# A two-level Strassen MLP on one core: first matmul in a written order of parts, sums begun in PSUM, second level in four products

## The chip, the core and the metric

The kernel runs on one core of one Trainium2 chip. The metric is the device time of one launch in microseconds (us); of three runs of the kernel before, the median was 1485.96 us (1485.87 to 1487.07). The profile shown below is one more execution of the same program, with the span between its first and last instruction.

## What is computed

```python
x: (8, 1024, 1024)   w1: (1024, 4096)   w2: (4096, 1024)      # float32
h = x @ w1
h = 0.5 * h * (1 + np.tanh(np.sqrt(2 / np.pi) * (h + 0.044715 * h ** 3)))
return (h @ w2).astype(np.float32)
```

An MLP block: 8192 rows, a first matmul with a hidden width of 4096, GELU, a second matmul. Operands are cast to float16, sums are kept in float32.

## The kernel before

**Tiling.** The 8192 rows go in eight stages (`sb` 0 to 7) of 1024 rows. A stage is `matmul1` (x times w1, GELU, result kept in SBUF as four blocks `g11, g12, g21, g22`) and then the second matmul (`matmul2_made` in stages 0 and 1, `matmul2` from stage 2 on). Each matmul is a Strassen-Winograd product over a 2x2 split of its operands: seven products of half-size blocks, named 1 to 7, instead of eight. The operands of the products are blocks or sums of blocks; the tables `W_SUM` and `S_SUM` say which. In the second matmul of stages 2 to 7 every product is itself split once more in the same way (class `Inner`, 7 x 7 parts), so its matmuls are 256 columns wide instead of 512.

**First matmul.** The hidden width is walked in eight pairs `j` of two 128-column chunks (`h` = 0 and 1). A pair has the seven products, each 4 matmuls of 512 columns for each chunk, 8 in all. From stage 2 on, products 2 and 3 (`INNER_1`) have a second level: seven parts of two 256-column matmuls, 14 in all, named here by their part `r`. The sums of the rows that this needs (`xs.inner[2]`, `xs.inner[3]`) are made on VectorE (DVE), four additions for each product; for product 3 that is done in the first pair (`more`). The matching sums of w1 were made in stage 1 (`inner_sums`), stored in DRAM (`in1_d`), and come back with the pair's other operands in `StoredHalf`, nine loads of 256 KB for each pair.

**How a pair's result is put together.** Product 1 goes to bank A and ScalarE (ACT) copies it to SBUF (`a`). Product 2 goes to its own bank, or part by part to a bank `z`, and DVE adds it to `a`, part by part (five or six additions of 256 columns) and then once more for each chunk. Product 6 is accumulated on bank A, ACT copies A again (`t`), product 7 is accumulated on A and added to the copy `p5` of product 5, product 4 is accumulated on A, and product 3 is added to `t`. ACT applies GELU to each of the four results of each chunk. At the end DVE subtracts g11 - g21 for the second matmul (`difference`).

**What sets the order.** TensorE (PE), ACT and DVE instructions are pinned to the order in which the Python code writes them (`keep_in_program_order`), so each of these engines is a queue: an instruction that waits holds up what stands behind it. All matmuls are issued from few lines: L438 (first matmul), L910 (`Inner.multiply`), L951 (`matmuls2`). All additions of DVE are issued from `tt` (L119), ACT's copies from `act_copy` (L135), GELU from L451. Loads go through SyncE's DMA queue (SP), stores and the cast of the next rows through GpSimd's (POOL). PSUM has 8 banks, taken by `psum()`; the framework lets one engine at a time into a bank, in the written order, and a new tile gets one when an old tile's last reader is done. SBUF tiles come from pools: `up` (26 tiles named `u`), `gcp` (4 named `gc`), `tp` (named `tmp`).

**Stage 1** has no second level in its first matmul. While it runs, DVE makes the next quarter's w1 sums (`MadeQuad.sum`, `inner_sums`), POOL stores them, and the raw blocks of the next quarter are read back by the four loads of `MadeQuad.__init__` (L168). These DVE jobs were run after the pair's own work: in pair 0 all of them behind the last addition of the pair (`half = 3 if j % 2 else 0`).

**End of a second matmul.** `FILL_2` makes the next stage's row sums on DVE while PE works; the last of them is `n3` (`37:n3`), run after product 3's last step, so it ends when the next first matmul has already begun. `i2` makes `xs.inner[2]` (`46:i2`).

Of the kernel before, what the change touches and what calls it, by code (L numbers as in the profile page):

```python
# [8 lines left out]
F32 = mybir.dt.float32  # L9
DT = mybir.dt.float16  # L10
GT = mybir.dt.float16
GELU = mybir.ActivationFunctionType.Gelu_apprx_tanh
ADD = mybir.AluOpType.add
# [8 lines left out]
SUMS = tuple(W_SUM)  # L22
BLOCKS = ("11", "21", "12", "22")
STEPS = (1, 2, 6, 5, 7, 3, 4)
INNER_1 = (2, 3)
HALF_ORDER = (1, 2, "s2", 5, 6, 3, "s3", 7, 4)
SPLIT_IN_M1 = (2, 3)


def slots(table):  # L30
# [6 lines left out]
    ;50:w60 w61;51:w62 w63;52:g30 g31;53:g32 g33  # L37
    ;60:w70 w71;61:w72 w73;62:w40 w41;63:w42 w43
    ;73:x5;40:x7 x6;41:x3 q5;42:q6 q7 q4
    ;43:i2 i3""".replace("\n    ", "")),  # L40
    slots("""10:g60 w50;11:g61 w51;12:g62 w52;13:g63 w53
    ;20:g50 p55;21:g51 p56;22:g52 p57;23:g53 p54
    ;50:w60 w61;51:w62 w63;52:g30 g31;53:g32 g33
# [12 lines left out]
    ;61:n5;63:a77;64:a76;65:a75;66:a73;67:n7  # L56
    ;71:y11 y12;72:y21 y22;73:a37;74:a36 w11;75:a35 w12;76:a33 w21;77:w22
    ;31:z11 z12;32:z21 z22;36:n6;37:n3""".replace("\n    ", ""))


@with_exitstack
def kernel(
# [27 lines left out]
    up = ctx.enter_context(tc.tile_pool(name="up", bufs=26))  # L90
    gp = ctx.enter_context(tc.tile_pool(name="gp", bufs=1))
    gcp = ctx.enter_context(tc.tile_pool(name="gcp", bufs=4))
    tp = ctx.enter_context(tc.tile_pool(name="tp", bufs=10))
    consts = ctx.enter_context(tc.tile_pool(name="consts", bufs=1))
    dram = ctx.enter_context(tc.tile_pool(name="dram", bufs=1, space=bass.MemoryType.DRAM))
    xdram = ctx.enter_context(tc.tile_pool(name="xdram", bufs=2, space=bass.MemoryType.DRAM))
# [3 lines left out]
    w2v = w2.rearrange("(a c p) (b o) -> b a p c o", a=2, p=P, b=2)  # L100

    w1_d = [dram.tile([P, 4, KH * QW], DT, name=f"w1_d{q}") for q in range(NI // QC)]
    in1_d = [dram.tile([P, 2, 2, KH * 2 * P], DT, name=f"in1_d{q}") for q in range(NI // QC)]
    raw_d = [dram.tile([P, 4, KH * QW], DT, name=f"raw_d{q}") for q in range(NI // QC)]
    in_d = {m: dram.tile([P, 4, NI // 2, OH // 2], DT, name=f"in_d{m}") for m in range(1, 8)}
    w2_d = [dram.tile([P, 4, QC * OH], DT, name=f"w2_d{q}") for q in range(NI // QC)]
# [2 lines left out]
    def psum():  # L109
        return pp.tile([P, HT], F32, name="ps")  # L110

    def temp():
        return tp.tile([P, HT], F32, name="tmp")

    def unit(rows, cols):
        return up.tile([P, rows, cols], DT, name="u")
# [1 line left out]
    def tt(out, in0, in1, op, pin=False):  # L118
        i = nc.vector.tensor_tensor(out=out, in0=in0, in1=in1, op=op)  # L119
        if pin:  # L120
            tc.keep_in_program_order(i)
# [12 lines left out]
    def act_copy(out, in_):  # L134
        tc.keep_in_program_order(nc.scalar.copy(out=out, in_=in_))  # L135
# [23 lines left out]
    class MadeQuad:  # L159


        def __init__(self, q, first, store):
            self.q, self.first, self.store = q, first, store
            self.raw = {b: unit(2 * KH, 2 * P) for b in BLOCKS}
            self.ops = {m: self.raw[b] for m, b in W_TERM.items()}
            if not first:
                for b in ("12", "11", "22", "21"):
                    nc.sync.dma_start(out=flat(self.raw[b]), in_=raw_d[q][:, BLOCKS.index(b), :])  # L168
# [44 lines left out]
                nc.gpsimd.dma_start(out=w1_d[self.q][:, SUMS.index(m), :], in_=flat(self.ops[m]))  # L213

        def inner_sums(self, m):
            t = self.ops[m].rearrange("p (h k c) (e n) -> p h k c e n", h=2, k=2, e=2)
            s = up.tile([P, 2, 4, 2, P], DT, name="u")

            def operand(b):
                if isinstance(b, int):  # L220
                    return s[:, :, list(S_SUM).index(b)]
                return t[:, :, int(b[1]) - 1, :, int(b[0]) - 1, :]

            for j, (u, op, v) in S_SUM.items():
                tt(operand(j), operand(u), operand(v), op, True)
            nc.gpsimd.dma_start(
                out=in1_d[self.q][:, INNER_1.index(m)].rearrange("p h n -> p (h n)"),
                in_=s.rearrange("p h j c n -> p (h j c n)"),
            )

        def chunk(self, m, c):
            return columns(self.ops[m], c % QC)
# [5 lines left out]
    def stored(d, raw, m):  # L238
        return raw[:, BLOCKS.index(W_TERM[m]), :] if m in W_TERM else d[:, SUMS.index(m), :]

    class StoredHalf:


        def __init__(self, i):
            q, h = divmod(i, 2)
            self.ops, self.sums = {}, {}
            n = KH * 2 * P
            for k, m in enumerate(HALF_ORDER):
                if k % 2 == 0:
                    two = up.tile([P, 2, n], DT, name="u")  # L250
                t = two[:, k % 2]
                if isinstance(m, str):
                    m = int(m[1])
                    self.sums[m] = t.rearrange("p (j c n) -> p j c n", j=4, c=2)
                    d = in1_d[q][:, INNER_1.index(m), h]
                else:
                    self.ops[m] = t.rearrange("p (k n) -> p k n", k=KH)
                    d = stored(w1_d[q], raw_d[q], m)[:, h * n:(h + 1) * n]
                nc.sync.dma_start(out=t, in_=d)

        def chunk(self, m, c):
            return self.ops[m][:, :, c % 2 * P:(c % 2 + 1) * P]

    class XOps(dict):
# [16 lines left out]
            for job in self.inner_jobs(m):  # L281
                job()

        def inner_jobs(self, m):
            self.inner[m] = up.tile([P, 4, 2, HT // 2], DT, name="u")

            def operand(b):
                if isinstance(b, int):
                    return self.inner[m][:, SUMS.index(b)]
                k, t = int(b[0]) - 1, int(b[1]) - 1  # L290
                return self[m][:, 2 * k:2 * k + 2, t * HT // 2:(t + 1) * HT // 2]

            return [lambda j=j, s=s: tt(operand(j), operand(s[0]), operand(s[2]), s[1], True)
                    for j, s in W_SUM.items()]

    def x_blocks():
        return {b: unit(KH, HT) for b in ("22", "21", "12", "11")}
# [8 lines left out]
    class First:  # L306
# [26 lines left out]
            load_in_order(flat(self.rows[a, q]), x2[r0:r0 + P, :])  # L333

        def cast(self, a, q):
            xn = tp.tile([P, 2, HT], DT, name="tmp")
            tc.keep_in_program_order(nc.vector.tensor_copy(out=xn, in_=self.rows[a, q]))
            self.rows[a, q] = xn

# [73 lines left out]
    def x_cast_paced(s, g_chunk, q, xb):  # L413

        mark = nc.gpsimd.tensor_copy(out=pace, in_=g_chunk[:, :2])  # L415
        return x_cast(s, mark, range(q * P, (q + 2) * P, P), xb)
# [15 lines left out]
    def matmul1(xs, sb, quads, start=None):  # L432
# [109 lines left out]
        for j in range(NI // 2):  # L542
# [10 lines left out]
                continue  # L553
            jobs = list(ahead(j))
            banks_a = [psum(), psum()]
            a = [temp(), temp()]
            for h in range(2):
                product(banks_a[h], source, 1, cs[h], True)
                act_copy(a[h], banks_a[h])
            banks_c, p5, t = [], [], [temp(), temp()]  # L560

            def five(h):
                if len(p5) == h:
                    banks_c.append(psum())
                    p5.append(temp())
                    product(banks_c[h], source, 5, cs[h], True)
                    act_copy(p5[h], banks_c[h])

# [108 lines left out]
        blocks = nxt.get("blocks")  # L677
        return g, early, nxt.get("xb") if blocks is None else XOps(blocks)

    def store(sb, b, q, src, **kw):
# [16 lines left out]
    def matmul2_made(sb, g, keep_w1, xb):  # L699
# [74 lines left out]
        def post(m, q, bank):  # L774
            if m in (1, 5, 6):
                t = {1: a, 5: p5, 6: t6}[m]
                t[q] = temp()
                act_copy(t[q], bank)
            elif m == 4:
                c = temp()  # L780
                act_copy(c, bank)
                store(sb, "21", q, c)
            else:
                t = {2: a, 3: t6, 7: p5}[m][q]
                tt(t, t, bank, ADD, True)
                at[q] = store(sb, {2: "11", 3: "12", 7: "22"}[m], q, t)
# [8 lines left out]
        for m, name, first in (  # L795
            (1, "a", True), (2, "b", True), (5, "c", True), (6, "a", False),
            (3, "c", False), (7, "a", False), (4, "a", False),
        ):
            for q in range(NQ):
                if first:  # L800
                    banks[name].append(psum())
                bank = banks[name][q]
                matmuls2(bank, s2[q] if m == 6 else rows(g[operands[m]], q), pieces(m), first)
                post(m, q, bank)
                if (m, q) == (5, 0) and sb == 0:
                    xb = x_cast(sb + 1, nc.gpsimd.tensor_copy(out=pace, in_=p5[0][:, :2]))
                if (m, q) == ((5, 0) if sb else (6, NQ - 1)):
                    xs = XOps(x_transpose(xb, load_in_order))
                    keep("22")
                if (m, q) == (3, NQ - 1) and sb == 0:  # L810
                    quad = MadeQuad(0, False, True)
                if (m, q) == (4, 0) and sb:
                    quad = StoredHalf(0)
                if (m, q) == (1, NQ - 1) and sb == 0:
                    sums[5] = [unit(2, HALF) for _ in range(NI // QC)]
                    for t in sums[5]:
                        act_copy(t[:, 0, :1], warm)
                    bring("22", act_copy, True)
                    keep("21")
                    keep("12")  # L820
                run((m, q))
# [206 lines left out]
            for n in products[m].steps(into[m]):  # L1028
                run((m, n))

    idle = consts.tile([P, HT], DT, name="idle")
    nc.vector.memset(idle, 0.0)
    warm = consts.tile([P, 1], F32, name="warm")
    pace = consts.tile([P, 2], DT, name="pace")
# [2 lines left out]
    first = First()  # L1037
    xs, quads = first.xs, [first.quad]
    for sb in range(NSB):
        g, early, nxt = matmul1(xs, sb, quads, first if sb == 0 else None)  # L1040
        if sb < 2:
            xs, quads = matmul2_made(sb, g, None if sb else quads[-1].keep_raw, nxt)
            continue
        matmul2(sb, g, early, nxt)
        if nxt is not None:
            xs, quads = nxt, [StoredHalf(0)]


# [28 lines left out]
```

## Time and profile before

| | us |
|---|---|
| median of three runs | 1485.96 |
| span of the profiled execution | 1485.0 |
| PE busy, of the span | 1476.1 |
| DVE busy | 1146.3 |
| ACT busy | 613.5 |
| POOL busy | 225.3 |
| first matmul of stage 2, its 544 matmuls (from 402.7) | 94.0 |
| first matmul of stage 4 (762.2 to 856.3), PE busy | 94.04 |
| the same, DVE busy | 68.66 |
| the same, ACT busy | 60.14 |
| DMA: read 355.47 MB, written 111.15 MB, over the span | 314 GB/s |

A page of the profile has for each engine the time in which it was busy; PE's time counts overlapping matmuls once. The view of chains follows what ended last back from step to step; a line there is a start, a length and a group of instructions. The timeline merges equal instructions that follow each other; a bracket tells how long the engine was idle before and what ended that. In the view of groups a row has a shape, its count, total time and the mean of one in ns. In the matmul groups the mean is longer than the spacing of two matmuls, because they are pipelined; the spacing is read from long stretches in the chain.

### The profile page before, as it was taken

The page shows a single profiled execution, that of the slowest core. Times are in us where ns is not written, and L with a number is a line of the kernel's source. Part 1 is how long each engine was busy: PE and PEld are TensorE (multiplying, and loading weights), DVE is VectorE, ACT ScalarE, POOL GpSimd, SP SyncE. Part 2 cuts the span into 40 slices and gives each one's busy share as a digit, 9 for nine tenths or more (in the row PEclk, how much of TensorE's full clock was granted, in tenths as well). Part 3 has the DMA queues.
Part 4 walks back from the last instruction along what each step waited for, and adds up shares of the span by engine and source line. Part 5 has one row for each costly group of instructions (what it writes and reads, how often), then busy time and mean ns, then how long its engine had stood idle before and what let it go on. Part 6 is the DMA issues. An engine that isn't in the chain of part 4 may idle for free.

```text
span 1485.0 us, 26324 instructions
## 1 busy us (share of the span) xinstructions
PE 1476.1 (99%) x9879; PEld 962.5 (65%) x9879; DVE 1146.3 (77%) x1792; ACT 613.5 (41%) x1154; POOL 225.3 (15%) x311
## 2 busy tenths in 40 slices
PE   8999999999999999999999999999999999999998
PEld 4444444444455787558875588655886568855687
DVE  5657458767677899779987799877997779877787
ACT  5665126621166412663136621366214652056510
POOL 1541122222201012100022001210111101101011
PEclk9999999999999999999999999999999999999999
DMA  9999898987997999999999999998999989997886
GB/s 323 345 345 394 224 360 287 405 274 228 379 292 169 359 304 309 319 214 387 325 295 337 218 372 313 307 305 234 376 292 326 303 263 341 295 370 245 295 277 213
DMA packets 242719, 453.70 MB, mean 306 GB/s; under 512 B 80672, under 2 KB 85792, under 8 KB 241696
## 3 DMA queue, kind: packets, MB, share of 16 engines
q1 hardware_dynamic: 215680, 358.69, 71.6%
q0 software_dynamic: 26912, 93.34, 21.5%
q8 instruction: 77, 1.26, 0.3%
q14 instruction: 50, 0.41, 0.1%
HBM read 355.47 MB, written 111.15 MB: 314 GB/s over the span
## 4 chain that ended last, share of the span: by engine, by line
PE 96%; DMA 2%; DVE 1%; ACT 0%; SPq 0%; issue 0%; DVEq 0%
PE ps L438 48%; PE ps L910 35%; PE ps L951 13%; PE ps L368 1%; DVE tmp L119 1%; DMA gc<-in_w_dram 1%; DMA u<-in_d 1%; DMA u<-w_d 1%; DMA u<-raw_d 0%; ACT tmp L135 0%; SPq L132 0%; PE ps L345 0%; DVE u L196 0%; DVE u L119 0%; DVE u L356 0%
## 5 line engine op out<-in xcount | busy, mean ns | idle before, releaser
L438 PE MATMUL ps<-u 128*128 128x512 f16 (+1 forms) x4104 | 746.6, 344 | 0.5 <-DMA u<-w_d 0.2
L119 DVE TENSOR_TENSOR tmp<-tmp,ps 128x256 f32<-128x256 f32 (+1 forms) x930 | 450.8, 532 | 263.3 <-PE ps L438 166.5
L438 PEld LDWEIGHTS <-u 128*128 128x128 f16 x4104 | 400.8, 98 | 343.7 <-issue 9.4
L135 ACT COPY tmp<-ps 128x512 f32<-128x512 f32 x410 | 231.2, 581 | 300.1 <-PE ps L438 153.9
L451 ACT ACTIVATE g<-tmp 128x512 f16<-128x512 f32 x378 | 238.1, 633 | 162.8 <-DVE tmp L119 162.7
L910 PE MATMUL ps<-u,gc 128*128 128x256 f16 x2688 | 300.4, 273 | 0.0
L910 PEld LDWEIGHTS <-gc 128*128 128x128 f16 x2688 | 262.5, 98 | 31.2
L119 DVE TENSOR_TENSOR u<-u 128x2048 f16<-128x2048 f16 (+3 forms) x292 | 217.8, 785 | 21.2 <-DMA raw_d<-u 11.4
L910 PE MATMUL ps<-u,g 128*128 128x256 f16 x2016 | 227.9, 273 | 0.0
L135 ACT COPY u<-ps 128x512 f32<-128x512 f32 (+1 forms) x134 | 78.0, 587 | 348.9 <-PE ps L910 341.4
L910 PEld LDWEIGHTS <-g 128*128 128x128 f16 x2016 | 197.3, 98 | 24.1
L119 DVE TENSOR_TENSOR u<-u,ps 128x512 f32<-128x512 f32 x216 | 147.8, 684 | 34.7 <-PE ps L910 28.5
L697 POOL DMA_DIRECT2D out_dram<-u x70 | 64.0, 989 | 710.5 <-issue 366.0
L951 PE MATMUL ps<-u,g 128*128 128x512 f16 x768 | 166.4, 379 | 0.0
L951 PEld LDWEIGHTS <-g 128*128 128x128 f16 x768 | 75.2, 98 | 90.6
L119 DVE TENSOR_TENSOR g<-g,g 128x2048 f16<-128x2048 f16 (+1 forms) x136 | 128.8, 969 | 1.6 <-ACT g L451 1.6
L119 DVE TENSOR_TENSOR gc<-g,gc 128x2048 f16<-128x2048 f16 x84 | 102.4, 1219 | 0.6
L119 DVE TENSOR_TENSOR gc<-g 128x2048 f16<-128x2048 f16 x78 | 95.0, 1218 | 0.0
L451 ACT ACTIVATE g<-ps 128x512 f16<-128x512 f32 x134 | 79.9, 597 | 15.1 <-PE ps L438 7.9
L138 POOL CAST u<-gc 128x1024 f16<-128x1024 f32 x40 | 45.4, 1141 | 69.5 <-DMA gc<-in_w_dram 56.4
L536 POOL TENSOR_TENSOR gc<-g 128x2048 f16<-128x2048 f16 x6 | 24.4, 4063 | 61.9 <-ACT g L451 61.9
L415 POOL COPY pace<-g 128x2 f16<-128x2 f16 x24 | 4.4, 185 | 190.1 <-ACT g L451 190.1
(37 smaller groups left out, 249.3 us busy)
## 6 DMA issues: line engine op xcount, KB each, us to landing
u<-w_d SPq DMA_DIRECT2D x336, 256.0 KB, 6.6
u<-in_d SPq DMA_DIRECT2D x168, 512.0 KB, 7.1
u<-raw_d SPq DMA_DIRECT2D x252, 256.0 KB, 7.1
out_dram<-u POOLq DMA_DIRECT2D x70, 512.0 KB, 9.2
gc<-in_w_dram SPq DMA_DIRECT2D x48, 512.0 KB, 6.3
u<-in_d SPq DMA_DIRECT2D x96, 256.0 KB, 6.8
raw_d<-u SPq DMA_DIRECT2D x32, 512.0 KB, 8.7
u<-raw_d SPq DMA_DIRECT2D x32, 512.0 KB, 13.9
```

What stands on the lines that cost most here:

```text
L119: i = nc.vector.tensor_tensor(out=out, in0=in0, in1=in1, op=op)
L135: tc.keep_in_program_order(nc.scalar.copy(out=out, in_=in_))
L138: pool_last[0] = nc.gpsimd.tensor_copy(out=out, in_=in_)
L368: tc.keep_in_program_order(nc.tensor.matmul(bank[:, cols], lhsT=w[:, k, :], rhs=self.xs.blocks[f"{a}{r}"][:, k, cols], start=r == 1 and k ...
L415: mark = nc.gpsimd.tensor_copy(out=pace, in_=g_chunk[:, :2])
L438: tc.keep_in_program_order(nc.tensor.matmul(bank, lhsT=w, rhs=x, start=first and k == 0, stop=k == n - 1, skip_group_check=not first,))
L451: gelu_last[0] = nc.scalar.activation(out=g[b][:, c, :], in_=src, func=GELU)
L536: nc.gpsimd.tensor_tensor(out=early[7], in0=u, in1=v, op=SUB)
L697: return nc.gpsimd.dma_start(out=rows, in_=src, **kw)
L910: tc.keep_in_program_order(nc.tensor.matmul(bank[:, i * OH // 2:(i + 1) * OH // 2], lhsT=t[:, c, i * P:(i + 1) * P], rhs=self.y[j][:, c, : ...
L951: tc.keep_in_program_order(nc.tensor.matmul(pair(bank), lhsT=a[:, c, :], rhs=chunks(pieces[c // QC])[:, :, c % QC, :], start=(first and c ...
```

## The change

Stage 0 keeps `matmul1`. Stages 1 to 7 use a new function, `matmul1_seeded`, which takes its order from written tables: `ORDER_PLAIN` in stage 1, and from stage 2 on `ORDER_HEAD` for pair 0, `ORDER` for pairs 1 to 6, `ORDER_TAIL` for pair 7. An entry is an operation and a key; all pairs' entries are sorted by 1000 j + key, so that pairs overlap: part 5 of product 1 (`P1r5`) of a pair comes at key -255, before the end of the pair ahead. `Pmchb` is half b (two matmuls of 512 columns) of product m for chunk h, `Pmrn` is part n (two matmuls of 256 columns) of a product with the second level, `J` runs jobs of DVE from a list until 1.2 of their written costs are used up, `gxyh` is a GELU.

Products 1, 5, 2 and 3 now have the second level (`INNER_1 = (1, 5, 2, 3)`), but in the pair of `ORDER_HEAD` only product 2. Sums no longer go through SBUF where a bank can hold them: ACT or DVE writes the start of a sum into a bank, and the matmuls that follow accumulate on it (`skip_group_check`, `start=False`). Of w1's second-level sums only those of products 1 and 2 are stored in DRAM (`STORED_1`); those of 3 and 5 are made by POOL from the loaded operands (`make_sums`), eight additions of 128x256 for each pair, issued when the pair before begins. POOL also takes over `difference`. In stage 1 the second-level sums of the first quarter move from the end of stage 0 (`43:i2 i3` of `FILL`) into pairs 0 and 1. `temp` tiles become pairs of half the number.

```diff
-INNER_1 = (2, 3)
-HALF_ORDER = (1, 2, "s2", 5, 6, 3, "s3", 7, 4)
+INNER_1 = (1, 5, 2, 3)
+STORED_1 = (1, 2)
...
+ORDER_PLAIN = order("""P1c10:-104 P1c11:-46 P1c00:-14 P1c01:13 P5c00:22 J:62 J:97 J:142 b1:167 J:222 b0:227 P5c10:233
+    P5c01:272 J:307 P5c11:313 p51:342 P6c10:395 P6c11:407 w1:413 p50:424 P6c00:424 P6c01:461 w0:499
+    P2c00:511 P2c10:513 P2c01:526 P3c10:550 J:556 P3c00:564 P3c01:616 J:672 P7c00:704 P7c10:715
...
+ORDER_HEAD = order("""J:-1385 P1c10:-1332 P1c11:-1168 J:-1152 P1c00:-1041 P1c01:-1039 a1:-953 P2r5:-773 a0:-627 P2r1:-592
+    P5c00:-480 P5c10:-400 P5c01:-302 P6c00:-240 P6c01:-196 J:-160 P6c10:-111 J:-106 p50:170 acc_2:211
+    q11_2:227 P2r6:278 P5c11:303 J:330 P6c11:342 w0:343 P3c00:354 q12_2:356 J:405 P3c01:417 p51:429
...
+ORDER = order("""P1r5:-255 P1r1:-201 q11_1:-134 P1r2:-80 s5_1:-76 P1r6:-72 P5r5:-7 q12_1:6 P5r1:10 P1r7:18 P1r3:20
+    q11_5:166 s5_5:184 P5r2:194 P5r6:195 q2x_1:195 P1r4:203 a0:204 P2r5:204 q12_5:225 P6c00:229 P5r7:236
...
+        def make_sums(self):
+            for m, s in self.sums.items():
...
+                for j, (u, op, v) in S_SUM.items() if m not in STORED_1 else ():
+                    tc.keep_in_program_order(nc.gpsimd.tensor_tensor(
+                        out=operand(j), in0=operand(u), in1=operand(v), op=op
+                    ))
...
+        bank_of = {1: "A", 6: "A", 7: "A", 4: "A", 2: "B", 5: "C", 3: "C"}
+        out_of = {"11": "B", "12": "C", "21": "A"}
...
+                if plain:
+                    self.source = quads[j // 2]
+                    self.jobs = ahead(j) + splits.pop(j, [])
+                    return
+                for i in range(len(quads), min(j + 3, npair)):
+                    quads.append(StoredHalf(i, table(i)))
...
+                if j == 0:
+                    for m in INNER_1:
+                        if m not in xs.inner:
+                            pool = (gcp, "gc") if m in (1, 5) else (up, "u")
+                            self.jobs += [(0.42, job) for job in xs.inner_jobs(m, *pool)]
...
+            def add(self, what, m):
+                m = int(m)
+                z, name = self.z[m], bank_of[m]
+                if m in (1, 5):
+                    i = 1 if m == 1 else 2
+                    if what == "s5":
+                        act_copy(seed[:, i], z[:, right])
+                    elif what == "q11":
+                        act_copy(self.bank(name, 0)[:, left], z[:, left])
+                    base = {"q12": seed[:, i], "q2x": seed[:, 0:i + 1:i]}
+                else:
+                    t = self.tmp("a" if m == 2 else "w")
+                    if what == "acc":
+                        tt(t[:, :, right], t[:, :, right], twice(z[:, right]), ADD, True)
+                    base = {"q11": t[:, 0, left], "q12": t[:, 0, right], "q2x": pair(t[:, 1])}
...
+                if what == "q2x":
+                    tt(pair(self.bank(name, 1)), base[what], twice(z[:, left]), ADD, True)
+                else:
+                    half = left if what == "q11" else right
+                    tt(self.bank(name, 0)[:, half], base[what], z[:, left], ADD, True)
...
+            def move(self, what, h):
+                if what == "p5":
+                    act_copy(self.tmp("p5")[:, h], self.bank("C", h))
+                    return
+                A = self.bank("A", h)
+                if what == "a":
+                    act_copy(self.tmp("a")[:, h], A)
+                elif what == "b":
+                    act_copy(self.bank("B", h), A)
+                else:
+                    p5 = self.tmp("p5")[:, h]
+                    out = p5 if what == "v" else self.tmp("w")[:, h] if 3 in self.inner else self.bank("C", h)
+                    tt(out, p5, A, ADD, True)
...
+        def ahead(j):
+            q, second = divmod(j, 2)
+            jobs = []
+            if j < 2:
+                jobs += quads[0].inner_jobs(STORED_1[j])
...
+            if not second:
+                quads.append(MadeQuad(q + 1, False, True))
+            quad = quads[q + 1]
+            jobs += [(1.2, lambda m=m: quad.sum(m, pin=True)) for m in ((7, 4) if second else (5, 6))]
+            jobs += quad.inner_jobs(STORED_1[second])
+            return jobs
```

## The prediction

> **What bounds the kernel now.** I read the shares of the engines, then the chain that ended last in order of time, then DVE's timeline where the chain leaves PE, then the rows by shape, then the loads of stage 1.
>
> ```profile
> PE 1476.1 (99%) x9879; PEld 962.5 (65%) x9879; DVE 1146.3 (77%) x1792; ACT 613.5 (41%) x1154; POOL 225.3 (15%) x311
> PE 96%; DMA 2%; DVE 1%; ACT 0%; SPq 0%; issue 0%; DVEq 0%
> ```
>
> PE is busy for 99% of the span and holds 96% of the chain: taken-away matmuls shorten the span, and every new wait of PE lengthens it.
>
> ```profile
> 209.28 96.69 PE ps L438 x448
> ...
> 496.70 85.63 PE ps L910 x784
> ...
> 588.83 1.96 DVE tmp L119 x4
> 590.79 0.04 issue
> 590.83 24.92 PE ps L438 x145
> ...
> 770.78 85.54 PE ps L438 x494
> 856.32 85.63 PE ps L910 x784
> ...
> 950.47 85.54 PE ps L438 x494
> ```
>
> Dense stretches give the spacing: 96.69/448 = 0.2158 us for a matmul of 512 columns, 85.63/784 = 0.1092 for 256. The stage from 770.78 to 950.47 takes 179.69. Its matmuls fill 320 x 0.2158 + (224 + 784) x 0.1092 = 179.1, so 0.55 us of a stage is gaps (one stage has 0.26 more, 590.83 to 770.78).
>
> ```profile
> 762.99 1.22 DVE L119 TENSOR_TENSOR u<-u 128x2048 f16<-128x2048 f16 x1
> 764.33 0.42 DVE L119 TENSOR_TENSOR tmp<-tmp,ps 128x256 f32<-128x256 f32 x1
> 764.67 0.88 DVE L119 TENSOR_TENSOR u<-u 128x512 f16<-128x512 f16 x2
> 765.90 0.75 DVE L119 TENSOR_TENSOR u<-u 128x512 f16<-128x512 f16 x2
> ```
>
> The first matmul of stage 4 begins at 762.11 (PE's timeline), but DVE is still at `n3` until 764.2, 2.0 us later with the overlap of its pipeline. Then come, one by one, four jobs of `xs.inner[3]`, 1.45 us in sum.
>
> **The change part by part.**
>
> *Matmuls.* A product on the first level costs 8 x 0.2158 = 1.727, on the second 14 x 0.1092 = 1.529: 0.198 less. In pairs 1 to 7 products 1 and 5 gain it (14 times), in pair 0 product 3 loses it: 13 x 0.198 = 2.57 a stage, stages 2 to 7: **-15.4**. Stages 0 and 1 keep their matmuls.
>
> *Old gaps.* They come from additions at places that the new order no longer has: 6 x 0.55 + 0.26: **-3.6**.
>
> *ACT and DVE in a middle pair.* Rows by shape:
>
> ```profile
> L119 DVE TENSOR_TENSOR tmp<-tmp,ps 128x512 f32<-128x512 f32 x402 | 260.3, 683 | 139.2 <-PE ps L438 78.2 <-PE ps L951 35.0 <-ACT tmp L135 14.7
> L135 ACT COPY tmp<-ps 128x512 f32<-128x512 f32 x410 | 231.2, 581 | 300.1 <-PE ps L438 153.9 <-PE ps L951 140.9 <-issue 1.7
> L119 DVE TENSOR_TENSOR tmp<-tmp,ps 128x256 f32<-128x256 f32 x528 | 200.4, 417 | 124.1 <-PE ps L438 88.3 <-ACT tmp L135 35.0
> L536 POOL TENSOR_TENSOR gc<-g 128x2048 f16<-128x2048 f16 x6 | 24.4, 4063 | 61.9 <-ACT g L451 61.9
> ```
>
> A pair becomes 3 x 1.727 + 4 x 1.529 = 11.30 us of PE. DVE had 11 additions of 256 and 6 of 512 columns and `difference`; it gets 6 and 10, by the rows 6 x 0.42 + 10 x 0.68 = 9.3. ACT has 8 GELUs, 4 copies of 512, 4 of 256: under 9. Both fit under 11.3, so what counts is the way back to PE. I walked the order of one pair with these durations. A matmul's result comes 0.16 after its slot (379 - 216 ns) and a hand-off takes 0.05. The tightest: `P1r6`, then `q12_1` on DVE, then `P1r7`, which writes the bank that `q12_1` reads: 0.16 + 0.42 + 0.05 = 0.63, covered by `P4c00`, `P5r5`, `P5r1` = 0.87. `P1r1`, `q11_1` on ACT, `P1r2`: at most 0.8 with the 512 row for the unseen copy of 256, covered by 1.09. So the walk has no wait, with 0.2 us to spare. No row has DVE or ACT writing PSUM. Bounds: below, the duration of the rows (PSUM read costs DVE nothing: 683 ns here against 686 from SBUF alone); above, a second access in series, the row's whole 0.42. I take the row, with one small gap of 0.05 for each of the 42 pairs, as each pair has now: **+2.1**. Banks: `z` and A, B, C live 83 us in sum for each pair (A alone 16 and 18), 83/11.3 = 7.3 of 8; in the walk a bank comes free just in time.
>
> *POOL and the loads.* A pair keeps its nine loads of 256 KB (pair 0 has eight), SP's queue is as long as before. POOL gets eight additions of 128x256 by 4063/2048 ns an element: 0.51 each, at most 0.7 with the 0.18 of POOL's smallest copy: 5.6; `difference` at half the 4.06 row: 2.0. Together 7.6 of 11.3, begun a pair ahead, so the pair ahead covers it: nothing on the path. In pair 0, where the cover is short, `s5` is made from a load that lands 11 to 12 us after the start, three additions later (14) just when `P5r5` of pair 1 comes (11.0 + 2.7). The casts of the next rows (L410), which stand behind `make_sums` in POOL's queue, go out some us later; their rows are wanted four pairs on. If an addition took over 1.1, POOL would set the pair.
>
> The trace shows POOL and DVE in each other's way: POOL's cast of 1024 columns is 1.04 alone and 1.38 to 1.50 while DVE adds SBUF to SBUF (28.0 to 37), and DVE's additions from PSUM keep their 0.68. In the new first matmuls of stages 2 to 7, DVE adds SBUF to SBUF only in pair 0. [...]
>
> *Pair 0 of stages 3 to 7.* `INNER_1` minus `i2` puts twelve row sums into the `J` entries, and all four filled `J` stand before `acc_2` and `q11_2` on DVE. DVE: free at 2.0, twelve jobs 3 x 1.45 = 4.4, `acc_2` 0.6, `q11_2` 0.4: done at 7.4. PE stands before `P2r6`, which writes the bank that `q11_2` reads, after ten halves of products 1, 5 and 6 (10 x 0.4316) and two parts (2 x 0.218): 4.75. Wait 2.7, nothing can pass it: **5 x 2.7 = +13.5**. Stage 2 has `i2`, `i3` from stage 1, eight jobs and a DVE that is free from the start: no wait (were DVE as late there as in stage 4, 1.2). In stages 3 to 7 the loads of pair 1 land 9 to 11 us after the start; `P1r1` of pair 1, now after 8.4 + 2.7, only just finds them, so less work on DVE alone would not win all of the 2.7 back.
>
> *Pair 0 of stage 1.* `J:97` holds `sum(5)` of the next quarter, `J:142` `sum(6)`; both stand before `w1`. They need raw blocks issued from 197.82 on, the second landing after 18.1 us, the third after 19.3:
>
> ```profile
> L168 SPq DMA_DIRECT2D u<-raw_d x4: 320/368/601, 197.8 to 201.6; - x4
> DMA to landing us min/median/max: 15.7/18.7/19.3
> ```
>
> Issued at 198.33 and 199.14 they land at 216.4 and 218.4, 7.1 and 9.1 after the stage's first matmul (209.28). Before, these sums ran behind the pair. One store of 512 KB less runs beside them (`i3` moves to pair 1); I take 0.6 off. DVE: `sum(5)` 6.5 to 7.65, `sum(6)` 8.5 to 9.65, four sums 1.35, `w1` 0.68: 11.7. PE wants `P3c10` (its bank is written by `w1`) after 15 halves, 6.5. Wait 5.2; bounds 0 (blocks there in time) and 5.9 (no store saved): **+5.3** with the hand-off. Pairs 2 and 4 have the same pattern, but their blocks are issued when buffers come free, in pair 1 and 3, and DVE runs 1.7 us ahead: 0 taken, 3 each as the bound.
>
> *Clock.* At the start the seven matmuls on `idle` (1.19 to 4.36) are spaced 0.43, half speed, and from 4.25 on the granted clock is 1.0; gaps up to 1.2 us between 4 and 13 did not lower it. A wait of 5.3 is longer than any gap the trace has after that. Bounds 0 and 3.2 at half speed, 1.6 lost; I take **+1.0**. [...]
>
> Sum against the profile's own span: 1485.0 - 15.4 - 3.6 + 2.1 + 13.5 + 5.3 + 1.0 = 1487.9. The median of the runs stands 1.0 above that span: **1489 us**.
>
> **Rivals.**
>
> *Stage 1 doesn't wait* (the raw blocks land early): it decides if the third block is there 3.3 us after the start, so that `sum(6)`, four sums and the end of `P6c11` leave `w1` done at 6.5; then 1489 - 6.3 = 1482.7. For it: these loads are not pinned, the framework may issue them sooner; against it: what stands before them in SP's queue is unchanged, and their 15.7 to 19.3 us are time in that queue. With half the head's wait gone too, 1476.
>
> *Hand-offs set the middle pairs.* The place is `P1r6`, `q12_1`, `P1r7` and its likes in 42 pairs; the price: DVE and ACT writing PSUM, or Tile's choice of banks, cost over 0.2 us more for each hand-off. Below that it is nothing. With 0.3, seven places of a pair are 0.1 to 0.26 late, 1.0 us a pair, 42 us; with 0.2, about 0.5 a stage, 3. For it: 7.3 of 8 banks, two waits on most instructions. Against it: reading PSUM costs the rows nothing. Likely size if it comes: +10, 1499; slower than before.
>
> *POOL late* (over 1.1 for an addition): each 0.1 above costs 0.8 a pair, 34 us in all. Against it: the 4063 row.
>
> *The change does not shorten PE*, because weight loads limit 256 columns: excluded by 0.1092 over 784 matmuls.
>
> **How the numbers follow.** My case, 1483 to 1494, likeliest 1489: 0.5. Stage 1 or pair 0 better than that, below 1483: 0.22. Hand-offs or banks: 0.2; POOL or loads: 0.08. A change within 0.2% (3.0 us, 1483.0 to 1488.9) can't be told from none; my case has half of itself on each side of 1489: same 0.26, slower 0.52, faster 0.22. Range 1477 to 1502; my case's own is 1483 to 1494.
>
> **What would show it.** Right: in each of stages 3 to 7 one PE gap of 2.5 to 3 us, 4.8 us after its first matmul, released by DVE; in stage 1 one gap near 215.7 released by DVE, which waits for `raw_d`; pairs 1 to 6 at 11.3 us each. Wrong: gaps in the middle pairs released by ACT or DVE, PE waiting for POOL, or no gap in stage 1.

## The result, and the profile after

The changed kernel takes 1502.1 us (median of 4 runs, 1499.1 to 1503.8) against 1486.5 before: a ratio of 1.0103, 95% interval 1.0089 to 1.0118. It is slower. The forecast was 1489 with a range up to 1502, so the time lies at the very top of it, and above the 1494 where the forecast's own case ended. The profiled execution is the shortest of the four: a span of 1497.3, which is 12.3 more than before.

The page first (engines' shares, then the chain by engine), and from the view of waits the line of PE's longest group: total, times, longest.

```profile
PE 1467.9 (98%) x10347; PEld 1011.6 (68%) x10347; DVE 1169.4 (78%) x1672; ACT 606.7 (41%) x1210; POOL 560.1 (37%) x703
PE 79%; DVE 4%; DMA 1%; issue 1%; SPq 0%; DVEq 0%
```

```profile
PE ps L821 <- DVE ps L152: 20.4, 9, 4.6
```

PE held 96% of the chain before and holds 79% now. All long waits of PE in these matmuls are for DVE: nine, of 20.4 us. Five of them are the ones in pair 0 of stages 3 to 7, four lie in stage 1. The timelines of PE, DVE and POOL in stage 1 (start, length, engine, operation, and in brackets the idle time before it and its releaser):

```profile
208.50 6.64 PE L821 MATMUL ps<-u 128*128 128x512 f16 x30
219.76 13.93 PE L821 MATMUL ps<-u 128*128 128x512 f16 x56 [4.62 <-DVE ps L152]
234.85 24.50 PE L821 MATMUL ps<-u 128*128 128x512 f16 x112 [1.16 <-DVE ps L152]
260.24 24.50 PE L821 MATMUL ps<-u 128*128 128x512 f16 x112 [0.89 <-DVE ps L152]
...
213.60 1.23 DVE L152 TENSOR_TENSOR u<-u 128x2048 f16<-128x2048 f16 x1 [6.37 <-DMA u<-raw_d]
216.41 2.69 DVE L152 TENSOR_TENSOR u<-u 128x2048 f16<-128x2048 f16 x5 [1.58 <-DMA u<-raw_d]
...
229.63 2.90 DVE L152 TENSOR_TENSOR u<-u 128x512 f16<-128x512 f16 x2
...
230.10 2.14 POOL L903 TENSOR_TENSOR g<-g,g 128x1024 f16<-128x1024 f16 x1
```

The wait that ends at 219.76 is the one forecast: `sum(5)` and `sum(6)` stand still until their raw blocks land. The one that ends at 234.85, in pair 1, is another: two additions of 0.42 us take 2.90, the second of them 2.56, and POOL's `difference` runs inside that.

Stages 3 to 7 in the chain of waits (start, length, what):

```profile
596.34 86.44 PE ps L821 x598
775.68 88.03 PE ps L821 x598
956.62 88.03 PE ps L821 x598
```

Each piece begins where the wait before `P2r6` ends, and each has the same 598 matmuls. The first takes 86.44, the others 1.59 more. Windows show why (busy time of PE, PEld, DVE, ACT and POOL, then the granted clock, `PEclk`, where 0.50 is half clock, then DMA's share and GB/s):

```profile
772.82:776.23 3.41, 0.84 (x6) 0.40 (x5) 3.38 (x10) 0.00 (x0) 0.00 (x0) 1.00 1.04 417
776.23:779.64 3.41, 3.41 (x12) 1.38 (x10) 1.03 (x2) 1.01 (x2) 1.08 (x2) 0.50 1.04 388
779.64:783.06 3.42, 3.42 (x24) 2.21 (x23) 1.90 (x3) 1.92 (x5) 3.34 (x6) 1.00 1.05 400
591.90:595.30 3.40, 1.87 (x9) 0.77 (x8) 3.33 (x11) 0.59 (x1) 0.00 (x0) 1.00 1.04 416
595.30:598.70 3.40, 2.36 (x14) 1.35 (x14) 2.61 (x6) 0.80 (x2) 0.00 (x0) 1.00 1.04 409
```

In stage 4 the whole wait of 2.73 us lies in 772.82 to 776.23, and the next 3.41 us run at half clock: 12 matmuls where 24 follow. In stage 3 the same wait is split between two such stretches, and the clock stays. The half-clock stretches of this execution begin at 776.23, 957.13, 1138.04 and 1318.95: 53 times 3.413 us apart, a fixed grid.

The parts in sum, where a matmul's slot is the spacing of two in a dense stretch (0.2158 and 0.1092 us) and a wait is counted from the end of the last slot:

| part of the span | forecast | in this execution |
|---|---|---|
| matmuls (sum of slots 1470.0 to 1454.6) | -15.4 | -15.4 |
| five waits before `P2r6` | +13.5 | +13.65 |
| half clock after them, 4 x 1.68 | 0 | +6.7 |
| stage 1, pair 0 | +5.3 | +4.78 |
| half clock after it | +1.0 | +1.7 |
| stage 1, odd pairs | 0 | +3.9 |
| old gaps, small gaps | -3.6 + 2.1 | -3.0 (what is left) |
| sum | +2.9 | +12.3 |

### The profile page after: what moved, and what is told of

The parts are those of the page before. It is cut to its first block, busy times and chain, and to the rows that moved or that the text cites. A ratio compares the mean times of both kernels' runs of the same rounds, so it can differ in the third digit from the quotient of the medians.

```text
span 1497.3 us, 27850 instructions
## 1 busy us (share of the span) xinstructions
PE 1467.9 (98%) x10347; PEld 1011.6 (68%) x10347; DVE 1169.4 (78%) x1672; ACT 606.7 (41%) x1210; POOL 560.1 (37%) x703
## 4 chain that ended last, share of the span: by engine, by line
PE 79%; DVE 4%; DMA 1%; issue 1%; SPq 0%; DVEq 0%
PE ps L821 40%; PE ps L1192 33%; PE ps L1233 6%; DVE u L152 2%; DMA u<-w_d 1%; DVE gc L152 1%; DVE tmp L152 0%; DVE ps L152 0%; SPq L318 0%; DVEq L152 0%
## 5 line engine op out<-in xcount | busy, mean ns | idle before, releaser
L821 PE MATMUL ps<-u 128*128 128x256 f16 (+1 forms) x3508 | 627.6, 328 | 20.4 <-DVE ps L152 20.4
L152 DVE TENSOR_TENSOR tmp<-tmp,ps 128x512 f32<-128x512 f32 x352 | 238.1, 685 | 127.6 <-PE ps L821 50.3
L168 ACT COPY tmp<-ps 128x512 f32<-128x512 f32 x282 | 163.8, 588 | 309.6 <-PE ps L821 150.8
L892 ACT ACTIVATE g<-ps 128x512 f16<-128x512 f32 x336 | 197.9, 601 | 106.4 <-PE ps L821 105.8
L329 POOL TENSOR_TENSOR u<-u 128x256 f16<-128x256 f16 x336 | 216.4, 670 | 51.6 <-DMA u<-w_d 19.5
L152 DVE TENSOR_TENSOR ps<-tmp,ps 128x256 f32<-128x256 f32 (+1 forms) x298 | 154.7, 532 | 38.4 <-PE ps L821 30.8
L903 POOL TENSOR_TENSOR g<-g,g 128x1024 f16<-128x1024 f16 x56 | 122.0, 2179 | 159.2 <-ACT g L892 159.1
L152 DVE TENSOR_TENSOR ps<-seed,ps 128x256 f32<-128x256 f32 (+1 forms) x168 | 94.5, 563 | 71.7 <-PE ps L821 69.3
L821 PE MATMUL ps<-gc,u 128*128 128x256 f16 x672 | 120.4, 273 | 0.0
L152 DVE TENSOR_TENSOR gc<-g,gc 128x2048 f16<-128x2048 f16 x84 | 114.0, 1357 | 3.1 <-PE ps L1192 3.1
```

What stands on the lines that cost most here:

```text
L329: tc.keep_in_program_order(nc.gpsimd.tensor_tensor(out=operand(j), in0=operand(u), in1=operand(v), op=op))
L821: tc.keep_in_program_order(nc.tensor.matmul(out, lhsT=w, rhs=x, start=first, stop=True, skip_group_check=not first,))
L892: gelu_last[0] = nc.scalar.activation(out=g[b][:, self.cs[h], :], in_=src, func=GELU)
L903: nc.gpsimd.tensor_tensor(out=g["21"][:, cs], in0=g["11"][:, cs], in1=g["21"][:, cs], op=SUB)
```

## The experiments

All are edits of the changed kernel; times are medians, "under" is against its 1502.1.

**head_fill.** Work in the wait, nothing else: `keep_clock` issues matmuls of 512 columns on zeros into a bank that nobody reads.

```diff
                 elif o[0] == "P":
+                    if self.j == 0 and o == "P2r6" and sb > 2:
+                        keep_clock(psum(), 12)
```

> Twelve matmuls of 512 columns on zeros, into a bank that nobody reads (no part of the computation), stand before P2r6 in pair 0 of stages 3 to 7: 12 x 0.216 = 2.6 us of work in the wait of 2.73. The order of everything else stays. Theory (the wait itself halves the clock): the wait for DVE ends at the same time (P2r6 within 0.2 us of 7.5 us after the stage's start), the half-clock stretches of 3.41 us after it in stages 4 to 7 are gone, the profile's span is 4 x 1.7 = 6.8 us under 1497.3, and the median, if ordinary runs drop the clock in all five stages and now and then elsewhere, 7 to 12 under 1502.1, with runs closer together than 1499.1 to 1503.8. Rival A (the clock falls for another reason, for example the load of the stage's start as a whole): the stretches stay, time as after or up to 2 us more. Rival B (no bank is free for them): P2r6 comes later by up to 2.6 us in each stage, time 1500 to 1510.

Measured: 1494.5 (1492.6 to 1495.2), ratio to before 1.0053 [1.0038, 1.0068], 7.6 under. PE's timeline in stage 4:

```profile
772.00 4.92 PE L823 MATMUL ps<-u 128*128 128x512 f16 x24
776.75 2.75 PE L375 MATMUL ps<-seed 128*128 128x512 f16 x12
779.48 3.62 PE L823 MATMUL ps<-u 128*128 128x256 f16 x20
```

`P2r6` comes 7.5 us after the stage's start as before (768.20 to 775.68 there), the real work waits as long, and no half-clock stretch is left in stages 2 to 7. So the wait made the clock fall, and the clock alone is worth 7.6 us in the median, about what four or five stretches of 1.7 give. The profiled span, 1493.4, is only 3.9 under, not the 6.8 expected: in this execution pair 0 of stage 1 waits 7.60 where it was 4.78, and half clock there lasts 10.24 us where it was 3.41.

**fill_some.** The same with `(2, 3, 4, 5, 6)[sb - 3]` matmuls in place of 12.

> Matmuls on zeros (no part of the computation) fill part of the wait of 2.73 us before P2r6: 2, 3, 4, 5 and 6 of 0.216 us in stages 3 to 7, so that 2.3, 2.1, 1.9, 1.65 and 1.45 us stay idle. Theory (the clock is judged in stretches of 3.41 us on a fixed grid, and the stretch after one that had more than about half of it idle runs at half clock; seen so far: 1.71 idle kept the clock, 2.20 lost it): stages 3 and 4 lose 3.41 us of clock if their idle time lies in one stretch of the grid, stages 6 and 7 lose none whatever the phase. Rival (the length of the wait counts, 2.7 us or more, not the grid): none of the five is at half clock. Rival (any wait over 1.4 us): all five are.

Measured (one execution): 1496.5. The windows of the grid around the waits of stages 3 and 4:

```profile
596.30:599.71 3.41, 1.40 (x7) 0.53 (x6) 3.38 (x10) 0.29 (x1) 0.00 (x0) 1.00 1.03 414
599.71:603.13 3.42, 3.30 (x9) 1.28 (x9) 1.79 (x4) 0.58 (x1) 0.49 (x1) 0.50 1.04 401
777.21:780.62 3.41, 1.65 (x8) 0.67 (x7) 3.36 (x9) 0.33 (x1) 0.00 (x0) 1.00 1.04 416
780.62:784.04 3.42, 3.26 (x20) 1.87 (x20) 2.42 (x5) 1.18 (x2) 0.61 (x1) 1.00 1.04 407
```

Of the five waits only stage 3's loses the clock. By the matmuls' slots (0.216 and 0.109 us) its stretch had 2.18 us without work; the highest that kept the clock was 2.14, in stage 1 of this execution, and stage 4 had 1.92. The stretches of the other kernels agree: 1.71 kept it, 2.20 and more lost it. Both rivals fall: a wait of 2.30 us was enough, one of 2.08 was not. No limit on the length of a wait fits, since the 2.73 of the changed kernel's stage 3, split by the grid, kept the clock. The expected "about half" was too low a limit: of 3.41 us, 2.14 without work kept the clock and 2.18 lost it.

**head_late.** Six row sums ahead of `q11_2` in place of twelve.

```diff
-... P6c01:-196 J:-160 P6c10:-111 J:-106 p50:170 ... P5c11:303 J:330 P6c11:342 ... q12_2:356 J:405 P3c01:417
+... P6c01:-196 P6c10:-111 p50:170 ... P5c11:303 P6c11:342 ... q12_2:356 P3c01:417
```

> Pair 0 of stages 2 to 7 keeps six row-sum jobs ahead of acc_2 and q11_2 instead of twelve; the other six run behind q2x_2 (entries J:584 and J:690). Theory (DVE's job list makes the wait, and a wait of 2.73 us also halves the granted clock for one stretch of 3.41 us): DVE reaches q11_2 2.2 us earlier, the wait before P2r6 falls from 2.73 to about 0.5 us, and no half-clock stretch is left in stages 4 to 7: span 5 x 2.2 + 4 x 1.7 = 17.8 us under the 1497.3 of the changed kernel's profile, about 1480; the median 18 to 22 under 1502.1. Rival A (the loads of pair 1, landing 9 to 11 us after the stage's start, come to the top): a new wait of 1 to 2.5 us before P1r5 or P1r1 of pair 1 in each of these stages, time 1490 to 1497. Rival B (DVE's late start from the stage before makes the wait, not the jobs): the wait stays over 2 us.

Measured: 1489.5, ratio 1.0019 [1.0009, 1.0028], 12.6 under. The wait before `P2r6` is 0.59 to 0.69, no clock is lost there: the theory is right on the cause, and rival B is out. Its size, 18 to 22 under, was missed: some 6 to 7 us later a second wait of 0.73 to 1.05 us has come, 4.5 us in five stages. In stage 6 the timelines of DVE and POOL show it:

```profile
1133.39 2.49 DVE L152 TENSOR_TENSOR u<-u 128x512 f16<-128x512 f16 x4
...
1134.07 2.97 POOL L329 TENSOR_TENSOR u<-u 128x256 f16<-128x256 f16 x4 [7.77 <-DMA u<-in_d]
```

Two of the four DVE additions took 0.42, the two that met POOL's additions 0.89, and `v0` stood behind them. POOL itself had begun when a load landed. In other stages PE's releaser is POOL or a load of pair 1: rival A has a part too.

**head_late2.** Also without `J:690` and `J:827`, so three of the six late jobs run at `J:1130`.

> As head_late, but of the six jobs behind q2x_2 three stand at J:584 and three at J:1130, in pair 1. Theory (the second wait of 0.7 to 1.05 us, 6 to 7 us after the first, is DVE's: two of its 0.42 us jobs took 0.89 beside GpSimd's additions and v0 stood behind six of them): it falls under 0.3 us, time 2 to 4 us under head_late's 1489.5. Rival (it is the loads of pair 1 and the additions that GpSimd makes of them): it stays at 0.7 to 1.0, time within 1 us of head_late.

Measured: 1488.5 (10 runs), ratio 1.0009 [1.0000, 1.0018]; the interval overlaps with that of head_late. The second wait is gone in stage 6, and 0.38, 0.87, 0.95 and 1.10 in the others, now put down to POOL's additions (one profiled execution of each kernel). Neither theory holds alone: DVE's jobs are a part, and POOL's sums of pair 1, begun when the loads land, set the rest. What share the loads have was not separated.

**diff_dve.** `difference` of stage 1 on DVE.

```diff
-                    nc.gpsimd.tensor_tensor(
-                        out=g["21"][:, cs], in0=g["11"][:, cs], in1=g["21"][:, cs], op=SUB
-                    )
+                    if plain:
+                        tt(g["21"][:, cs], g["11"][:, cs], g["21"][:, cs], SUB, True)
+                    else:
+                        nc.gpsimd.tensor_tensor(
...
```

> In stage 1 alone, the subtraction called difference runs on DVE again instead of GpSimd; order and everything else as in the changed kernel. Theory (GpSimd's 2.14 us subtraction of SBUF by SBUF holds DVE's SBUF addition that has begun, whole: five additions of 0.42 us took 2.56): these five are 0.42 again, w1 and w0 of pairs 1, 3 and 5 come 2.1 us earlier less 0.7 for the subtraction, the waits of 1.06 to 1.33 + 0.17 us in the odd pairs go, stage 1 is 3.9 us shorter; median 1498, if DVE's subtraction itself falls ahead of w1 about 1499. Rival (the odd pairs are late by the number of jobs ahead of w1, the four of 0.69 us on the split blocks among them): the waits stay at 1 us or grow by 0.7, time 1502 to 1504. The wait of 4.78 in pair 0 stays by both.

Measured: 1497.1, ratio 1.0077 [1.0062, 1.0092], 5.0 under. DVE's groups by shape in stage 1's first matmul (busy us, mean ns), the changed kernel, then this one:

```profile
L152 DVE TENSOR_TENSOR u<-u 128x512 f16<-128x512 f16 x28 | 21.3, 801 | 0.2
```

```profile
L152 DVE TENSOR_TENSOR u<-u 128x512 f16<-128x512 f16 x28 | 10.9, 419 | 0.2
...
L152 DVE TENSOR_TENSOR g<-g,g 128x1024 f16<-128x1024 f16 x7 | 4.8, 686 | 3.1 <-ACT g L892 3.1
```

Five of the 28 took 2.56 each, now all take 0.42, and the waits of pairs 1, 3 and 5 are gone, though DVE got 4.8 us of work more. The rival (too many jobs ahead of `w1`) is out.

**st1_late.** All `J` of stage 1 behind `w0` and `v1`.

```diff
-ORDER_PLAIN: ... P5c00:22 J:62 J:97 J:142 b1:167 J:222 b0:227 ... J:307 ... w0:499 ... J:556 ... J:672 ... v1:858
+even pairs:  ... P5c00:22 b1:167 b0:227 ... w0:499 J:500 ... v1:858 J:859 J:860 J:861 J:862 J:863
+odd pairs:   ... P5c00:22 b1:167 b0:227 ... w0:499 J:500 J:505 J:507 ... v1:858 J:859 J:860 J:861
```

> In stage 1 alone the J entries stand behind w1 and w0: in even pairs one behind w0 and five behind v1, in odd pairs three behind w0 and three behind v1. Theory (pair 0 waits because w1 stands behind sums of blocks that land 7 and 9 us after the stage's start): the wait of 4.78 us and the half-clock stretch of 1.7 us after it go, and the 3.9 us of the odd pairs too since w1 no longer stands behind the additions that GpSimd holds: 10.4 us less, span near 1487, median near 1492. Rival A (the sums are only moved to where something else waits for them: v0 behind the sum of a late block in pair 0, the products of the next quarter): up to 3 us of it come back. Rival B (GpSimd's subtraction still holds DVE 2.1 us and w1 of the next pair comes late): waits of about 1 us in four to six pairs, 5 us come back.

Measured: 1494.0, ratio 1.0056 [1.0040, 1.0072], 8.1 under. Stage 1's first matmul has no wait over 0.2 us left, so the theory is right there. But PE now waits 4.6 us ahead of the last 16 matmuls of stage 1's second matmul (the expectations further down call this place its start; it is its end). The timelines of PE and DVE:

```profile
361.16 38.15 PE L1238 MATMUL ps<-u,g 128*128 128x512 f16 x176
403.77 6.51 PE L1238 MATMUL ps<-u,g 128*128 128x512 f16 x16 [4.46 <-DVE tmp L157]
...
400.69 2.43 DVE L157 TENSOR_TENSOR u<-u 128x2048 f16<-128x2048 f16 x3 [14.47 <-DMA u<-xb]
```

The sixteen blocks of x for the next stage landed 9 to 28 us after their issue (median 20.6), where the changed kernel had 2.6 to 5.9 (4.4). DVE stands still for them, and the addition that PE needs stands behind. So rival A came, at a place that it did not name. What slows these loads was not settled.

**st1_pair0.** That edit of the even pairs in pair 0 alone (with `J:62` kept).

> Only in pair 0 of stage 1 the J entries with the sums of late blocks stand behind w0 and v1; the other pairs of stage 1 keep theirs. Theory (w1 behind sum(5) and sum(6) is the wait of 4.8 to 7.6 us; the late DVE jobs of the other pairs made the new wait in st1_late): pair 0 has no wait over 0.5 us, the half-clock stretch near 220 goes, the odd pairs keep their 1.06 to 1.33 + 0.17 us, and no wait appears at the start of stage 1's second matmul: 6.5 to 10 us under 1502.1, median 1492 to 1496. Rival (any delay of stage 1's buffers holds back the loads for the second matmul's start): 4 us or more there, median 1497 to 1500.

Measured: 1497.5, ratio 1.0074 [1.0060, 1.0088], 4.6 under where 6.5 to 10 were expected. No wait in the second matmul, and none over 0.2 us in pair 0; but pair 1 now waits 4.79 at 232.37. DVE's timeline:

```profile
220.36 10.03 DVE L157 TENSOR_TENSOR u<-u 128x2048 f16<-128x2048 f16 x15 [0.43 <-DMA u<-raw_d]
...
231.63 1.28 DVE L157 TENSOR_TENSOR ps<-tmp,ps 128x512 f32<-128x512 f32 x2
```

The jobs of pairs 0 and 1 stand in one piece of 10 us (with the 2.1 of `difference` in it) ahead of pair 1's `w1`. The theory was right on pair 0 and missed that the work moved out of it lands ahead of the next `w1`.

**best**: head_late2, diff_dve and st1_pair0 together. **best2**: the odd pairs' edit of st1_late in pair 1 as well.

> Three edits together: six row-sum jobs of pair 0 moved behind q11_2 (three at J:584, three at J:1130), difference of stage 1 on DVE, and the J entries with late blocks in pair 0 of stage 1 behind w0 and v1. Theory (the three waits are separate and the 15.5 us of matmuls are all there once they go): from the 1502.1 of the changed kernel, 12.6 for the head as measured in head_late, 2 to 3 more for the second wait of pair 0, 5.0 for difference, 6.5 to 10 for pair 0 of stage 1: 1472 to 1476 median, 0.7 to 1.0% under the kernel before. Rival A (what was moved in stage 1 delays the loads behind it, as in st1_late): 4 to 7 us come back at the start of stage 1's second matmul, 1478 to 1481. Rival B (the loads of pair 1 set the end of pair 0 in stages 3 to 7): the second wait of about 0.9 us stays, 1476 to 1479.

> As best, and in pair 1 of stage 1 too the J entries stand behind w0 and v1. Theory (in best the wait only moved on: the jobs of pairs 0 and 1, 11 us of DVE in one piece from 219.6 on, stood ahead of w1 of pair 1, 2.38 us for PE; moved behind w0 and v1 they fill DVE's free time of the next pairs): no wait over 0.6 us in stage 1, no half-clock stretch there, median 2.4 to 5 us under best's 1479.6, about 1475 to 1477. Rival A (the backlog moves on once more, to w1 of pair 2 or 3): a wait of 1 to 3 us there, median within 1.5 us of best. Rival B (blocks released later hold back the loads of the second matmul, as in st1_late): 3 to 5 us at its start, median 1478 to 1481.

Measured: best 1479.6 (5 runs), ratio 0.9953 [0.9939, 0.9966]; best2 1477.1 (5 runs, 1476.4 to 1477.6), ratio 0.9940 [0.9926, 0.9953]. Both beat both kernels. In best a wait of 2.38 stays in pair 1, in best2 one of 1.47 in pair 2: its rival A in part, since the median still falls by 2.5. The view of PE's waits in best2:

```profile
PE ps L831 <- DVE ps L162: 3.6, 7, 1.3
PE ps L831 <- POOL u L339: 1.8, 3, 1.1
```

DVE's part falls from 20.4 us to 3.6, and no half-clock stretch lies between the first matmuls and the last. best missed its 1472 to 1476 in part because the sum took the stage 1 part as one wait, not as a load that moves on; moving that load on gave 2.5. Its rival B has a part too: in its profile second waits of 0.84 and 0.92 us stay in two of the five stages, beside 0.59 before `P2r6` in each.

## Why the prediction was right and where it failed

**The sum.** The time is in the range by its width, which is luck: the upper part, to 1502, was for the rival with slow hand-offs (1499), and that one did not come. The working missed by two terms, below.

**Matmuls, old gaps, head waits.** Matmuls and head waits are right to 0.2 us each, and the old gaps are gone as forecast, for stage 5 closes with these terms: 179.69 - 2.57 - 0.55 + 2.73 + 1.7 (half clock) = 181.0; from 956.62 to 1137.56 it takes 180.94.

**Middle pairs.** The walk held: that sum leaves nothing for hand-offs, so the rival *hand-offs set the middle pairs* is out. DVE writing a bank costs 691 ns for 512 columns, 684 writing SBUF: the lower bound. A POOL addition took 670 ns (taken: 0.51 to 0.7), and PE waited for none in the changed kernel. The small gaps are 0.6 by what is left of the sum, not 2.1.

**Stage 1, pair 0.** Right in place and cause, 4.78 against 5.3. In the profiles of the kernels that keep this order it is 4.65 to 7.6, with the landing of the blocks; the rival *stage 1 doesn't wait* is out.

**The step that failed: no clock for the five waits of 2.7.** They cost four half-clock stretches, 6.7 us in the profile; head_fill takes 7.6 off the median. The sum has a term of clock for the 5.3 of stage 1 and none for these, though the trace before shows neither. PE's longest gap in it after the first 4.25 us is 0.93, or 1.1 counted from the end of the last slot:

```profile
8.41 0.62 PE L345 MATMUL ps<-identity,tmp 128*128 128x128 f16 x8 [0.93 <-DVE tmp L337]
```

That these waits cost no clock was the author's estimate, and not shown. Measured here, half clock came in whole stretches of 3.41 us on a fixed grid, after a stretch with 2.18 us or more without work, and not after one with 2.14 (fill_some). Also, the profiled execution lost it four times in five; the other three had spans 2.9 to 4.7 longer at a mean clock of 0.990 to 0.992 instead of 0.994. A clock lower by 0.002 to 0.004 over 1500 us is 6 to 12 us at half clock, 3 to 6 us lost: enough for the difference, but worked out, since those runs have no trace.

**The second: nothing for `difference` against DVE in stage 1.** Of the two in each other's way the text had one row, POOL's cast, 1.04 alone and 1.38 to 1.50 beside DVE's additions, and the sum has no term for the odd pairs. The trace of the changed kernel has 2.14 us of POOL, 2.14 us added to DVE's 0.42 and 3.9 us on the path in the odd pairs, and diff_dve gives 5.0 back. The row was half of the picture: it had POOL's cast slowed by a DVE addition that had begun first (at 27.83, the cast at 28.03). The same stretch of the trace before holds the other half, DVE's additions, which the text did not read:

```profile
29.82 1.05 POOL L138 CAST u<-gc 128x1024 f16<-128x1024 f32 x1 [0.40 <-DMA gc<-in_w_dram]
30.00 1.41 DVE L119 TENSOR_TENSOR u<-u 128x1024 f16<-128x1024 f16 x1
31.33 0.68 DVE L119 TENSOR_TENSOR u<-u 128x1024 f16<-128x1024 f16 x1
```

The cast that the text took as alone had DVE's addition beside it. Begun first, it kept its 1.05, and the addition took 1.41 in place of 0.68. `difference` in stage 1 meets DVE in this order. The pairs held as the bound, 2 and 4, have no wait: the waits come a pair later.

"Less work on DVE alone would not win all of the 2.7 back" proved right: head_late's second wait is 0.9 on average, with the loads of pair 1 as one part of it.

## What to carry to other kernels

Work that nobody needs yet should stand behind, not ahead of, the instruction that PE needs next on the same engine; but see what stands there for the pair after, since a backlog moves on. Here a PE wait of 2.73 us cost 1.6 to 1.7 us more by the clock (stages 4 to 7 of the changed kernel), or nothing (stage 3), by the luck of the grid; one of 2.30 lost the clock too (fill_some), and a long one cost more: after the 7.60 of head_fill's stage 1, matmuls ran 5.2 us at half clock, 2.6 lost by estimate. Where such a wait can't be removed, matmuls on zeros in it can pay (head_fill: 7.6 us). Before giving an addition to POOL, look for SBUF-to-SBUF additions of DVE that would meet it, and count up to its whole length for them (2.14 of 2.14 us in stage 1, 0.47 of 0.67 in head_late).

## What the runs showed that was not expected

The grid of 3.41 us, and the clock kept with 2.14 us without work and lost with 2.18 (fill_some). A stretch already at half clock stayed there with 0.93 us idle (st1_late, at 402.84), and one with 0.68 idle brought the clock back (st1_pair0, at 231.69). An estimate from these figures: if work at half clock is counted half, the 2.48 busy are worth 1.24 and the 2.73 are worth 1.37, and one limit fits both states, 3.41 - 2.16 = 1.25 with the middle of 2.14 and 2.18. No run tested that by itself.

A POOL addition of 670 ns added 0.47 to a DVE addition from SBUF (0.42 to 0.89, head_late in stage 6), and one of 2.59 us at the start of the second matmuls made 1.22 into 3.15 (at 504.93 and in five more stages of the changed kernel). DVE's additions with one operand in PSUM kept their time: 685 ns on average for 512 columns, 683 before, with POOL busy for 560.1 us in place of 225.3.
